# Eight small products moved into the scan's levels, two norms and one product order rearranged, and a small PSUM bank at two bank changes

## The chip, the cores and the metric

The kernel runs on one core of a Trainium2 chip. The metric is device time in microseconds (us) of one execution. Engines are named as in the profile: PE (TensorE, matmuls), PEld (its weight loads), DVE (VectorE), ACT (ScalarE), POOL (GpSimd) and SP (SyncE, whose queue carries most of the DMAs).

## The reference

One layer of a hybrid decoder for 1040 prompt tokens (16 learned meta tokens and 1024 more) and 8 sample tokens, all in float32, with model width 1024:

```
h += 0.5 * SwiGLU_1(rmsnorm(h))            # D_FF = 2816
u  = rmsnorm(h) @ w_in                     # columns shared by two groups of heads
HGRN2, 4 heads, key and value dim 128:
    f = lb + (1-lb) sigmoid(u_f); k = 1 - f; v = u_i; q = silu(u_q)
    S_t = diag(f_t) S_{t-1} + k_t v_t^T;   o_t = S_t^T q_t
    per-head RMSNorm(o) * silu(u_g)
Mamba-2, 8 heads of dim 64, state 128: conv(4) + SiLU, SSD scan, grouped RMSNorm
h += concat(hgrn_out, ssm_out) @ w_out
h += 0.5 * SwiGLU_2(rmsnorm(h))
y  = rmsnorm(h)
```

Outputs are y for prompt and samples and the new states of both groups. Each of the 8 samples has one token and a state of its own, so that its o is one 128x128 by 128x1 product per head.

## The kernel before

Every float32 product is made of three matmuls of split operands: each operand is a high part and a low remainder, and `mm3` issues high by high (L163), high by low (L164) and low by high (L165). PE's order is the order of the program in most of the kernel; in out_proj, and in the last head's norm before it, a scheduler places the instructions of all engines.

PSUM has eight banks. Four are small work banks (`K.psm()`, "mis" in the profile) and four are for accumulation (`K.psum()`, "acc"). In the second half of each FFN (`down`) the accumulation banks are used in twos for six of seven products and, for the last product, one by one, after `K.banks(1)`; the first box of that last product is the place called the bank change.

Both FFNs use a scheme of seven products of blocks in place of eight. `Blocks` makes the operands: `scaled` applies the norm's weight (ACT, L335), `sum_` adds blocks, `cast` makes the high part (ACT, L346), and `low` the remainder (DVE, L352). `w.hi` and `w.lo` (L462, L466), or `w.split` for both, do the same for weights. What is made when, beside which matmul, is written by hand: `before(S, n, ...)` puts calls ahead of step n of the pair of products that is being worked on, and the list which `first2` returns is the order of the seven products. L674, L676, L678, L683, L685 and L689 combine the products' banks.

`hgrn_scan` computes one head. It works through levels m = 1, 2, 4, 8, 16, 32 and 64; at each level there are small matmuls of m or 16 columns (L1758 at levels 32 and 64), then DVE's work for the next level, and then `fill(5)`, which puts five `mm3`, 15 wide matmuls of the next projections, into PE's order. The sample states are loaded and updated in two groups of four (`samples`, at levels 2 and 16). At the head's end PE does 16 output matmuls (L1854, L1856), two for the last 16 tokens (L1860, L1861) and the eight sample products (L1864), which share their bank `po8`. `hgrn_out` then takes the bank's contents as pieces: a square by ACT (L1875), the product with the gate by DVE (L1881), and the norm. For the last head the norm's column sums are matmuls with ones (L1890), taken out of their bank by ACT (L1891), and `rstd_wide` (L194 to L204) makes the root. L1893 applies it.

`out_proj` goes over 8 row tiles and 2 quarters of the tokens for each half of the tokens and each half of the operands: 12 matmuls per tile, a sum on DVE (L1912), and, where `after` is given, a square by ACT (L229) and a sum by POOL (L230) for FFN2's norm. Weights are split by L157 and L158. `Norm.end` (L237 and L173 to L185) finishes the norm of one quarter; `begin_half` (L254 to L256) and `finish` (L259 to L264) do it for two quarters together.

Of the kernel before, what the change touches and what calls it, by code (L numbers as in the profile page):

```python
# [17 lines left out]
P = 128  # L18
# [298 lines left out]
class Blocks:  # L317
# [7 lines left out]
        self.b[p] = self.K.slot("u", self.K.T)  # L325
        return self.b[p]

    def scaled(self, h, wcol, ps):

        for p in ps:  # L330
            k0, n = {1: (0, 0), 7: (0, 1), 2: (4, 0), 3: (4, 1)}[p]
            q = 2 * self.half + n
            t = self.new(p)
            for k in range(4):
                self.K.nc.scalar.activation(t[:, k * self.K.Q : k * self.K.Q + self.K.Q], h[k0 + k][:, q * self.K.Q : q * self.K.Q + self.K.Q], AF.Identity, scale=wcol[:, k0 + k : k0 + k + 1])  # L335

    def sum_(self, p):
# [517 lines left out]
def down(K, S, wdv, hidden, src, h, after):  # L855
# [82 lines left out]
    for a, p in enumerate(DORDER):  # L938
        b = s0 + 24 * a
        if a == 0:  # L940
            at = [b + k for k in (-14, -11, -11, -9, -9, -7)], [b + k for k in (-8, -7, -6, -5, -4, -2)]
        else:
            at = [b - 22 + 3 * m for m in range(6)], [b - 16 + 3 * m for m in range(6)]
        op = hidden.load(S, p, at)
        if a < 6:
            for j in range(KT // 2):
                box = []
                for g in range(3):
                    pieces(p, j, g, b + 6 * j + 2 * g, None)
                    for c in range(2):  # L950

                        def mm(p=p, j=j, g=g, c=c, op=op, box=box):
                            if not box:
                                box.append(K.psum2()[:, :, :K.Q])
                            matmuls(p, j, g, c, op, box[0][:, c])

                        S.add(mm, (lambda p=p, j=j, box=box: post(p, j, slice(0, 2), box[0])) if (g, c) == (2, 1) else None)
        else:
            S.before(b, lambda: K.banks(1))
            then = after(S, h, b - 48 + 24, b + 12, b + 24)  # L960
            for j in range(KT // 2):
                for g in range(3):

                    pieces(p, j, g, b + 3 * j + g, None if j < 2 else "u", (0, 0, 1, 2, 3, 4)[3 * j + g] if j < 2 else 0)
            for c in range(2):
                for j in range(KT // 2):
                    box = []
                    for g in range(3):

                        def mm(p=p, j=j, g=g, c=c, op=op, box=box):  # L970
                            if not box:
                                box.append(K.psum()[:, :K.Q])
                            matmuls(p, j, g, c, op, box[0])

                        S.add(mm, (lambda p=p, j=j, c=c, box=box: post(p, j, slice(c, c + 1), box[0][:, None])) if g == 2 else None)
# [696 lines left out]
def hgrn_scan(K, a, o, hd, u, fill):  # L1672
# [70 lines left out]


    load(0)
    copies, copies8 = [diagonal], [small_diagonal]
    fe = f
    for li, m in enumerate(LEVELS):
        nb = 64 // m
        w = TP if m < 16 else 1024  # L1750
        ps = K.psm()
        qv = qf[:, :1024].rearrange("p (c b s i) -> p c b s i", c=8, s=2, i=m)
        if m >= 32:

            for c in range(8):
                for b in range(nb):
                    r = slice(2 * m * b, 2 * m * b + m)
                    nc.tensor.matmul(ps[r, m * c : m * c + m], kg[:, P * c + 2 * m * b : P * c + 2 * m * b + m], qv[:, c, b, 1], start=True, stop=True)  # L1758
            for b in range(nb):
                r = slice(2 * m * b, 2 * m * b + m)  # L1760
                nc.scalar.copy(pv[r, :, 2 * m * b + m : 2 * m * b + 2 * m], ps[r, : 8 * m].rearrange("p (c i) -> p c i", c=8))
        else:
            nb = 16 // m
            for c in range(8):
                for j in range(4):
                    r = slice(32 * j, 32 * j + 32)
                    nc.tensor.matmul(ps[r, 16 * c : 16 * c + 16], kg[:, P * c + 32 * j : P * c + 32 * j + 32], qv[:, c, nb * j : nb * j + nb, 1], start=True, stop=True)  # L1767

            def copy(m=m, nb=nb, ps=ps):
                pvm = pd.rearrange("p c (b s i) -> p c b s i", s=2, i=m)[:, :, :, 1]  # L1770
                nc.vector.copy_predicated(pvm, K.mask[m].rearrange("p (b i) -> p b i", i=m)[:, None].broadcast_to([P, 8, nb, m]), ps[:, :P].rearrange("p (c b i) -> p c b i", c=8, i=m))
                if m == 16:
                    for r in range(0, P, 32):
                        nc.scalar.copy(pv[r : r + 32, :, r : r + 32], pd[r : r + 32])

            copies.append(copy)
        if li == 0:
            s8 = K.psm()
            nc.tensor.matmul(s8[:16, 64:80], kg[:, 1024:TP], q[:, 1024:TP], start=True, stop=True)
        if m < 16:  # L1780
            q8 = qf[:, 1024:TP].rearrange("p (b s i) -> p b s i", s=2, i=m)
            nc.tensor.matmul(s8[:16, 8 * li : 8 * li + 8], kg[:, 1024:TP], q8[:, :, 1], start=True, stop=True)

            def copy8(li=li, m=m):
                nc.vector.copy_predicated(p8.rearrange("p (b s i) -> p b s i", s=2, i=m)[:, :, 1], K.mask[m][:16, 0:8].rearrange("p (b i) -> p b i", i=m), s8[:16, 8 * li : 8 * li + 8].rearrange("p (b i) -> p b i", i=m))

            copies8.append(copy8)
        n = w // (2 * m)
        fv = fe[:, : w // m].rearrange("p (b s) -> p b s", s=2)
        qw = qf[:, :w].rearrange("p (b s i) -> p b s i", s=2, i=m)  # L1790
        kw = kg[:, :w].rearrange("p (b s i) -> p b s i", s=2, i=m)
        mid = 512 // (2 * m)
        for bs in (slice(0, mid), slice(mid, n)):
            k = bs.stop - bs.start
            nc.vector.tensor_mul(qw[:, bs, 1], qw[:, bs, 1], fv[:, bs, 0:1].broadcast_to([P, k, m]))
            nc.vector.tensor_mul(kw[:, bs, 0], kw[:, bs, 0], fv[:, bs, 1:2].broadcast_to([P, k, m]))
        fn = fp.tile([P, n])
        nc.vector.tensor_mul(fn, fv[:, :, 0], fv[:, :, 1])
        if m == 8:
            f16 = fn  # L1800
        fe = fn
        for copy in copies:
            copy()
        copies = []
        if m == 8:
            for copy in copies8:
                copy()
        if m == 4:
            load(4)
        if m in (2, 16):  # L1810
            samples({2: 0, 16: 4}[m])
        fill(5)
# [47 lines left out]
    nc.tensor.matmul(po8[:, 0:16], vt8, p8, start=True, stop=False)  # L1860
    nc.tensor.matmul(po8[:, 0:16], ss[:, 7], qf[:, 1024:TP], start=False, stop=True)  # L1861

    for b in range(NS):
        nc.tensor.matmul(po8[:, 16 + b : 17 + b], states[b // 4 * 4][:, b % 4], qs[:, b : b + 1], start=True, stop=True)  # L1864
    pieces.append((po8, 1024 - NM, 24))
    return pieces


def hgrn_out(K, hd, pieces, g, tag, fill):
# [12 lines left out]
    if hd < 3:  # L1882
        fill(14)
        next(steps, None)
    else:
        fill(5)
        for ps, c0, w in pieces:
            cs = slice(c0, c0 + w)
            pr = K.psum()
            nc.tensor.matmul(pr[:, :w], K.ones[1], v[:, cs], start=True, stop=True)  # L1890
            an = nc.scalar.activation(v[:, cs], pr[:, :w], AF.Identity, scale=1.0 / P, bias=K.eps)  # L1891
        rstd_wide(K, v, r, an)
# [146 lines left out]
def body(ctx, tc, a, o):  # L2039
# [200 lines left out]
    def keep2(half):  # L2240
        for k in range(KT):
            cs = slice(half * 2 * K.Q, half * 2 * K.Q + 2 * K.Q)
            nc.sync.dma_start(hd2[k][:, cs], h[k][:, cs])

    def after2(k, q):
        nf2.add(k, q)
        if k == KT - 1 and q < 2:
            nf2.end(q)
            if q == 1:
                keep2(0)  # L2250

    out_proj(K, a, h, 1, opb, 0, after2)
    out_proj(K, a, h, 0, opa, 1)
    out_proj(K, a, h, 1, opb, 1, after2)
    ops2 = [Blocks(K, i) for i in range(2)]

    def first2(S, w):
# [29 lines left out]
        e.sum_(5)  # L2287
        e.low(1)
        e.cast(5)
        w.split(2)  # L2290
        e.low(5)
        w.split(6)
        w.split(7)
        w.split(3)
        before(S, 1, (e.scaled, h, wn2, (2,)))
        before(S, 2, (e.scaled, h, wn2, (3,)), (e.cast, 2))
        before(S, 3, (e.sum_, 6), (e.low, 2), (nf2.begin_half, 1))
        before(S, 4, (e.cast, 6), (e.sum_, 7))
        before(S, 5, (e.low, 6), (e.cast, 7))
        before(S, 6, (e.low, 7), (e.sum_, 4), (e.cast, 3))  # L2300
        before(S, 7, (nf2.finish, (1, 1)))
        before(S, 8, (e.low, 3), (e.cast, 4))
        before(S, 9, (w.hi, 4))
        before(S, 10, (e.low, 4), (keep2, 1), (w.lo, 4))
        return 1, 5, 2, 6, 7, 3, 4

    def after3(S, h, e3, e0, e1):
        nf = []
# [55 lines left out]
```

## Time and profile before

| | us |
|---|---|
| median of 3 runs | 1956.12 |
| lowest and highest | 1952.58, 1958.87 |
| profiled execution | 1959.24 |
| its span | 1957.5 |

The profile is of one execution; times in it count from the span's start. PE is the busiest engine by far. In the lists, `x` gives the number of instruction records (a float32 matmul on 32-bit operands may leave two), and the clock is what was granted to TensorE, as a share of full speed. FFN1 lies up to about 690 us, the four heads' scans lie between 930 and 1170 us, out_proj from 1174 to 1276 us, and FFN2 follows.

### The profile page before, as it was taken

To read this page: it belongs to the slowest core of one execution; us is meant where nothing else is said; L and a number is where in the kernel's file an instruction comes from. 1 tells how busy PE (TensorE), PEld (TensorE's weight loads), DVE (VectorE), ACT (ScalarE), POOL (GpSimd) and SP (SyncE) were. 2 spreads that over 40 slices of the span, in tenths; PEclk is the share of its full clock that TensorE was granted. 3 is DMA by queue.
4 is the path that set the end of the run, shared out by engine and by line. 5 is a ranking of instruction groups with operands and counts; after the bars stand their busy time and mean duration, and the time that the engine had idled before them with its cause. 6 is when DMAs were issued, how large, how long until landed. Compare 5 with 4: busy or idle time off the path is not lost.

```text
span 1957.5 us, 41043 instructions
## 1 busy us (share of the span) xinstructions
PE 1917.1 (98%) x16569; PEld 1883.5 (96%) x16569; DVE 1532.7 (78%) x2783; ACT 850.3 (43%) x1632; POOL 91.5 (5%) x155
## 2 busy tenths in 40 slices
PE   7999999999999999999999999999999999999997
PEld 6999999999999999999999999999999999999997
DVE  7788888888788867576765657888888888878965
ACT  7533233333533644466644535742332323354353
POOL 4000000000000410000000001200000000000000
PEclk9999999999999999999999999999999999999999
DMA  7223333335977551221641454224332333587862
GB/s 222 77 88 109 93 99 105 100 97 161 283 234 251 158 159 51 66 87 44 177 122 52 124 172 135 77 82 120 92 109 87 103 104 104 161 245 233 271 194 77
DMA packets 324646, 260.59 MB, mean 133 GB/s; under 512 B 17824, under 2 KB 299680, under 8 KB 324448
## 3 DMA queue, kind: packets, MB, share of 16 engines
q1 hardware_dynamic: 324216, 257.92, 43.5%
q8 instruction: 131, 2.15, 0.5%
q14 instruction: 59, 0.48, 0.1%
q0 software_dynamic: 224, 0.04, 0.0%
q10 hardware_dynamic: 16, 0.00, 0.0%
HBM read 192.90 MB, written 65.07 MB: 132 GB/s over the span
## 4 chain that ended last, share of the span: by engine, by line
PE 86%; DVE 7%; DMA 2%; ACT 2%; issue 1%; SPq 0%; POOL 0%; DVEq 0%; ACTq 0%; POOLq 0%
PE acc L163 26%; PE acc L165 25%; PE acc L164 25%; PE mis L163 1%; PE mis L165 1%; PE mis L164 1%; DVE u L352 1%; DVE ws L466 1%; DMA s<-in_x_prompt_dram 1%; DMA r<-in_w_ffn_up_dram 1%; DVE r L458 1%; PE mis L1767 1%; DMA s<-cumd 1%; PE mis L1835 0%; DVE t L669 0%
## 5 line engine op out<-in xcount | busy, mean ns | idle before, releaser
L163 PE MATMUL acc<-u,ws 128*128 128x258 f32 (+3 forms) x4248 | 1243.1, 293 | 7.5 <-DVE t L683 2.5
L164 PE MATMUL acc<-u,ws 128*128 128x258 f32 (+3 forms) x4248 | 1233.2, 290 | 4.4 <-DVE u L352 4.0
L165 PE MATMUL acc<-u,ws 128*128 128x258 f32 (+3 forms) x4248 | 1232.6, 290 | 3.3 <-DVE ws L466 3.3
L163 PEld LDWEIGHTS acc<-u,ws 128*128 128x128 f32 x4248 | 805.1, 190 | 12.9 <-issue 3.6
L164 PEld LDWEIGHTS acc<-u,ws 128*128 128x128 f32 x4248 | 807.5, 190 | 6.9 <-DVE u L352 5.0
L165 PEld LDWEIGHTS acc<-u,ws 128*128 128x128 f32 x4248 | 804.9, 189 | 4.7 <-DVE ws L466 4.6
L466 DVE TENSOR_TENSOR ws<-r,ws 128x512 fp32r<-128x512 f32 x276 | 190.9, 693 | 75.0 <-ACT ws L462 74.9
L462 ACT CAST ws<-r 128x512 fp32r<-128x512 f32 x276 | 160.1, 615 | 12.9 <-ACT ws L462 7.7
L458 DVE TENSOR_TENSOR r<-r,r 128x512 f32<-128x512 f32 x176 | 120.9, 689 | 4.8 <-DMA r<-in_w_ffn_up_dram 3.3
L681 ACT ACTIVATE t<-t 128x516 f32<-128x516 f32 (+1 forms) x41 | 26.2, 639 | 213.3 <-DVE t L669 213.3
L712 ACT ACTIVATE t<-t 128x524 f32<-128x524 f32 (+1 forms) x47 | 29.9, 639 | 196.3 <-DVE t L669 196.3
L846 DVE TENSOR_TENSOR u<-u,u 128x1048 fp32r<-128x1048 f32 (+3 forms) x84 | 97.0, 1157 | 5.5 <-ACT u L842 5.5
L669 DVE TENSOR_TENSOR t<-t,u 128x524 f32<-128x524 f32 (+1 forms) x135 | 92.9, 697 | 2.9
L158 DVE TENSOR_TENSOR ws<-r,ws 128x512 fp32r<-128x512 f32 x88 | 60.6, 699 | 42.2 <-ACT ws L157 41.9
L230 POOL TENSOR_TENSOR t<-t,t 128x262 f32<-128x262 f32 (+1 forms) x56 | 54.4, 982 | 812.5 <-ACT t L229 708.5
L903 ACT CAST ws<-u 128x512 fp32r<-128x512 f32 (+1 forms) x72 | 42.2, 586 | 102.2 <-DVE u L898 92.1
L842 ACT CAST u<-u 128x1048 fp32r<-128x1048 f32 (+3 forms) x84 | 82.9, 989 | 0.0
L932 DVE SCALAR_TENSOR_TENSOR s<-acc,s 128x524 f32<-128x524 f32 (+3 forms) x88 | 54.6, 643 | 31.7 <-PE acc L165 31.4
L903 ACT CAST ws<-r 128x512 fp32r<-128x512 f32 (+1 forms) x84 | 47.9, 582 | 70.8 <-DVE r L898 29.5
L908 DVE TENSOR_TENSOR ws<-r,ws 128x512 fp32r<-128x512 f32 (+1 forms) x84 | 57.4, 693 | 23.2 <-ACT ws L903 23.1
L157 ACT CAST ws<-r 128x512 fp32r<-128x512 f32 x88 | 53.9, 617 | 36.5 <-PE acc L165 30.6
L908 DVE TENSOR_TENSOR ws<-u,ws 128x512 fp32r<-128x512 f32 (+1 forms) x72 | 47.4, 658 | 26.5 <-ACT ws L903 26.5
(435 smaller groups left out, 2290.7 us busy)
## 6 DMA issues: line engine op xcount, KB each, us to landing
r<-in_w_ffn_down_dram SPq DMA_DIRECT2D x128, 256.0 KB
hd<-s SPq DMA_DIRECT2D x93, 258.0 KB
r<-in_w_ffn_gate_dram SPq DMA_DIRECT2D x88, 256.0 KB
r<-in_w_ffn_up_dram SPq DMA_DIRECT2D x88, 256.0 KB
hd<-s SPq DMA_DIRECT2D x77, 262.0 KB
u<-hd SPq DMA_DIRECT2D x36, 516.0 KB
u<-hd SPq DMA_DIRECT2D x28, 524.0 KB
r<-in_w_in_dram SPq DMA_DIRECT2D x56, 256.0 KB
```

What stands on the lines that cost most here:

```text
L158: self.nc.vector.tensor_sub(lo, src, hi.bitcast(F32))
L163: mm(ps, whi, xhi, start=first, stop=False, skip_group_check=more)
L164: mm(ps, whi, xlo, start=False, stop=False, skip_group_check=more)
L165: mm(ps, wlo, xhi, start=False, stop=last, skip_group_check=more)
L458: self.K.nc.vector.tensor_tensor(self.raw[p], self.raw[x], self.raw[y], op)
L462: self.K.nc.scalar.copy(self.w[p][:, : self.n * P], self.raw[p])
L466: self.K.nc.vector.tensor_sub(t[:, 512 : 512 + w], self.raw[p], t[:, :w].bitcast(F32))
L669: nc.vector.tensor_mul(t, t if src is None else src, spread.lanes(i, cs))
L842: K.nc.scalar.copy(hi, lo.bitcast(F32))
L846: K.nc.vector.tensor_sub(lo, lo.bitcast(F32), hi.bitcast(F32))
L903: nc.scalar.copy(w[p, j, g][:, : n * P], src)
L908: nc.vector.tensor_sub(t[:, 512 : 512 + n * P], box[0], t[:, : n * P].bitcast(F32))
```

## The change

There are five parts. The eight sample products are done by a new function `outputs(b0)` in two groups of four, behind the matmuls of level 32 and of level 64, each group in a small bank of its own, and ACT copies them to a tile `os8` in SBUF; `hgrn_out` then has four pieces in place of three. In the last head's norm the ones-matmuls write to small banks. FFN2's norm for the first half of the tokens is begun and finished for both quarters together, inside the next call of out_proj. FFN2's first pair has another product order, its scalings can be made in parts (`ks`), and some splits stand at other steps. The first box of the last product in `down` uses a small bank.

```diff
-    def scaled(self, h, wcol, ps):
+    def scaled(self, h, wcol, ps, ks=range(4)):
...
-            t = self.new(p)
-            for k in range(4):
+            t = self.new(p) if 0 in ks else self.b[p]
+            for k in ks:
...
-                                box.append(K.psum()[:, :K.Q])
+                                box.append((K.psum() if c or j else K.psm())[:, :K.Q])
...
     load(0)
+    os8 = small("os8", P, NS)
+
+    def outputs(b0):
+        ps = K.psm()
+        for i in range(4):
+            nc.tensor.matmul(ps[:, i : i + 1], states[b0][:, i], qs[:, b0 + i : b0 + i + 1], start=True, stop=True)
+        nc.scalar.copy(os8[:, b0 : b0 + 4], ps[:, 0:4])
+
...
+        if m >= 32:
+            outputs({32: 0, 64: 4}[m])
         n = w // (2 * m)
...
-    for b in range(NS):
-        nc.tensor.matmul(po8[:, 16 + b : 17 + b], states[b // 4 * 4][:, b % 4], qs[:, b : b + 1], start=True, stop=True)
-    pieces.append((po8, 1024 - NM, 24))
+    pieces.append((po8, 1024 - NM, 16))
+    pieces.append((os8, TP - NM, NS))
...
-            pr = K.psum()
+            pr = K.psm()
             nc.tensor.matmul(pr[:, :w], K.ones[1], v[:, cs], start=True, stop=True)
...
     def after2(k, q):
         nf2.add(k, q)
-        if k == KT - 1 and q < 2:
-            nf2.end(q)
-            if q == 1:
-                keep2(0)
+        if (k, q) == (KT - 1, 1):
+            keep2(0)
+
+    def norm2(k, q):
+        if (k, q) == (0, 3):
+            nf2.begin_half(0)
+        elif (k, q) == (1, 2):
+            nf2.finish((0, 0))
 
     out_proj(K, a, h, 1, opb, 0, after2)
-    out_proj(K, a, h, 0, opa, 1)
+    out_proj(K, a, h, 0, opa, 1, norm2)
     out_proj(K, a, h, 1, opb, 1, after2)
...
+        w.split(6)
+        e.low(5)
+        e.scaled(h, wn2, (2,), (0, 1))
         w.split(2)
-        e.low(5)
-        w.split(6)
-        w.split(7)
-        w.split(3)
-        before(S, 1, (e.scaled, h, wn2, (2,)))
-        before(S, 2, (e.scaled, h, wn2, (3,)), (e.cast, 2))
-        before(S, 3, (e.sum_, 6), (e.low, 2), (nf2.begin_half, 1))
+        e.scaled(h, wn2, (2,), (2,))
+        before(S, 1, (e.scaled, h, wn2, (2,), (3,)), (w.hi, 7), (e.scaled, h, wn2, (3,), (0, 1)), (w.lo, 7))
+        before(S, 2, (w.hi, 3), (e.scaled, h, wn2, (3,), (2, 3)), (e.cast, 2))
+        before(S, 3, (w.lo, 3), (e.sum_, 6), (e.low, 2), (nf2.begin_half, 1))
...
-        before(S, 6, (e.low, 7), (e.sum_, 4), (e.cast, 3))
-        before(S, 7, (nf2.finish, (1, 1)))
+        before(S, 6, (e.low, 7), (e.sum_, 4))
+        before(S, 7, (e.cast, 3), (nf2.finish, (1, 1)))
...
-        return 1, 5, 2, 6, 7, 3, 4
+        return 1, 5, 6, 2, 7, 3, 4
```

How the instructions stand now is shown at three places, in each engine's own order; line numbers of the changed kernel are some 8 to 13 higher in these functions (L1864, L1866, L1870 and L1871 are the old L1854, L1856, L1860 and L1861).

PE at the end of a head (the third), before: the output matmuls in bank 13391, then those of `po8` (13400), `qs` being the samples' q and `r` their states.

```order
L1854 MATMUL mis_13391<-s_12838,s_12796 128x128
L1856 MATMUL mis_13391<-s_12794,s_13315 128x128
L1860 MATMUL mis_13400<-p_1606_12840,vt_1598_12797 128x16
L1861 MATMUL mis_13400<-s_12794,s_13315 128x16
L1864 MATMUL mis_13400<-qs_12818,r_12877 128x1 x4
L1864 MATMUL mis_13400<-qs_12818,r_13047 128x1 x4
L163 MATMUL acc_13367<-u_8461,ws_13124 128x350
```

PE at level 64 of the same head in the changed kernel: L1766 is the level's own matmul, L1751 the sample product.

```order
L165 MATMUL acc_13223<-u_8461,ws_12795 128x350
L1766 MATMUL mis_13272<-s_12808,u_12042 64x64 x8
L1751 MATMUL mis_13282<-qs_12832,r_13062 128x1 x4
L163 MATMUL acc_13223<-u_8462,ws_12795 128x350
L164 MATMUL acc_13223<-u_8470,ws_12795 128x350
```

The four products of the second group have moved from the end of the head to a place between the level's matmuls and the wide ones of the filling; the first group stands in the same way at level 32.

PE at the last head's norm, before: L163 to L165 into bank 14165 are the last projection, those into bank 14268 the first tile of out_proj.

```order
L165 MATMUL acc_14165<-u_8463,ws_13508 128x344
L1890 MATMUL acc_14224<-u_14216,ones_83 128x496
L1890 MATMUL acc_14227<-u_14216,ones_83 128x512
L1890 MATMUL acc_14230<-u_14216,ones_83 128x24
L163 MATMUL acc_14268<-u_13567,ws_14260 128x258
```

The same norm in the changed kernel (L1899); bank 14327 is out_proj's third tile.

```order
L165 MATMUL acc_14327<-u_13588,ws_14291 128x258
L1899 MATMUL mis_14252<-u_14242,ones_83 128x496
L163 MATMUL acc_14327<-u_13830,ws_14291 128x258
L164 MATMUL acc_14327<-u_13831,ws_14291 128x258
L165 MATMUL acc_14327<-u_13830,ws_14291 128x258
L163 MATMUL acc_14327<-u_14018,ws_14296 128x258
L1899 MATMUL mis_14255<-u_14242,ones_83 128x512
L1899 MATMUL mis_14258<-u_14242,ones_83 128x16
L164 MATMUL acc_14327<-u_14019,ws_14296 128x258
```

The ones-matmuls, which stood ahead of all of out_proj, now come after its first 27 matmuls and between later ones.

ACT at FFN2's first pair, before: L674 and L678 copy banks that PE has filled, L335 scales a block of 258 tokens, and L346 casts.

```order
L674 COPY t_15589<-acc_15576 128x258
L335 ACTIVATE u_15591<-s_14250,col 128x258
L335 ACTIVATE u_15591<-s_14252,col 128x258
L335 ACTIVATE u_15591<-s_14254,col 128x258
L335 ACTIVATE u_15591<-s_14256,col 128x258
L335 ACTIVATE u_15609<-s_14250,col 128x258
L335 ACTIVATE u_15609<-s_14252,col 128x258
L335 ACTIVATE u_15609<-s_14254,col 128x258
L335 ACTIVATE u_15609<-s_14256,col 128x258
L346 CAST u_15614<-u_15591 128x1032
L678 COPY t_15628<-acc_15576 128x258
```

ACT there in the changed kernel; L462 casts weights, and 15591 and 15616 are the blocks that were 15591 and 15609.

```order
L335 ACTIVATE u_15591<-s_14285,col 128x258
L674 COPY t_15611<-acc_15598 128x258
L335 ACTIVATE u_15591<-s_14287,col 128x258
L462 CAST ws_15614<-r_15494 128x512
L335 ACTIVATE u_15616<-s_14281,col 128x258
L335 ACTIVATE u_15616<-s_14283,col 128x258
L462 CAST ws_15633<-r_15560 128x512
L335 ACTIVATE u_15616<-s_14285,col 128x258
L335 ACTIVATE u_15616<-s_14287,col 128x258
L346 CAST u_15637<-u_15591 128x1032
```

Three of the eight scalings now stand ahead of the first copy L674, and the casts of two weights between the others.

## The prediction, made before the changed kernel ran

> **What bounds the kernel now.** I read the page first. The profiled execution took 1959.24 us, and its span is 1957.5 us, so 1.7 us lie outside the span; the median of the three timed runs, 1956.12 us, lies 3.1 us below this execution.
>
> ```profile
> span 1957.5 us, 41043 instructions
> PE 1917.1 (98%) x16569; PEld 1883.5 (96%) x16569; DVE 1532.7 (78%) x2783; ACT 850.3 (43%) x1632; POOL 91.5 (5%) x155
> ```
>
> TensorE (PE) is busy in 1917.1 of 1957.5 us, so all that can be had without dropping matmuls is the 40.4 us in which it stands still, and whatever makes the matmuls themselves slow. A change that leaves the products as they are, as this one does, can act on nothing else. For the second kind I cut the ends of the four HGRN2 heads into windows and read the granted clock. Columns: window, length, PE busy (records), clock as a share of full speed, DMA share, GB/s.
>
> ```profile
> 964.45:967.86 3.41, 3.41 (x14) 0.50 1.02 272
> 1056.60:1060.01 3.41, 3.41 (x24) 1.00 0.02 5
> 1107.81:1111.22 3.41, 3.41 (x14) 0.50 0.12 47
> 1159.00:1162.42 3.42, 3.42 (x31) 1.00 0.77 233
> 1162.42:1165.83 3.41, 3.41 (x14) 0.50 1.02 401
> 1165.83:1169.24 3.41, 3.41 (x23) 1.00 1.01 396
> ```
>
> Three of the four heads are followed by one window of 3.41 us at half clock. The starts stand on one grid: 1107.81 - 964.45 is 42.0 windows and 1162.42 - 1107.81 is 16.0. The timeline of PE around the same four ends (start, duration, operation) shows what precedes them.
>
> ```profile
> 961.99 0.39 PE L1860 MATMUL mis<-p,vt 16*128 16x16 f32 x2
> 964.34 0.54 PE L163 MATMUL acc<-u,ws 128*128 128x344 f32 x1
> ...
> 1054.54 0.39 PE L1860 MATMUL mis<-p,vt 16*128 16x16 f32 x2
> 1056.89 0.40 PE L163 MATMUL acc<-u,ws 128*128 128x344 f32 x1
> ...
> 1104.99 0.39 PE L1860 MATMUL mis<-p,vt 16*128 16x16 f32 x2
> 1107.35 0.40 PE L163 MATMUL acc<-u,ws 128*128 128x350 f32 x1
> ...
> 1160.18 0.39 PE L1860 MATMUL mis<-p,vt 16*128 16x16 f32 x2
> 1160.75 2.03 PE L1864 MATMUL mis<-qs,r 128*128 128x1 f32 x16
> 1162.64 0.63 PE L163 MATMUL acc<-u,ws 128*128 128x344 f32 x1
> ...
> 1163.65 0.49 PE L163 MATMUL acc<-u,ws 128*128 128x344 f32 x1
> 1164.51 0.49 PE L163 MATMUL acc<-u,ws 128*128 128x344 f32 x1
> ...
> 1166.06 0.32 PE L163 MATMUL acc<-u,ws 128*128 128x344 f32 x1
> 1166.53 0.32 PE L163 MATMUL acc<-u,ws 128*128 128x344 f32 x1
> ```
>
> From L1860 to the next wide matmul PE does only products 1 or 16 columns wide, for 2.35 us (961.99 to 964.34; 2.35, 2.36 and 2.46 in the others). The wide matmuls left in the window ahead of the half-clock one fill 3.41 less the narrow stretch inside it: 961.04 to 961.99 and 964.34 to 964.45 make 1.06 us in head 0; 1.05 in head 2; 1159.00 to 1160.18 make 1.18 in head 3. In head 1 the grid cuts the stretch at 1056.60: the window from 1053.19 has 1.35 us of wide matmuls, and no half clock follows. So in these four a window with up to 1.18 us of wide work cost the clock, and one with 1.35 did not. The price: three matmuls take 0.86 us at half clock (1163.65 to 1164.51) and 0.47 at full (1166.06 to 1166.53), so a window of 3.41 us does the work of 1.86 and costs 1.55 us.
>
> **The change, part by part.**
>
> *Sample products at two levels.* The eight products (16 records of L1864, some 1.8 us of PE) leave the head's end; four go behind level 32's matmuls and four behind level 64's. PE's work is the same. What stands there now, in head 3:
>
> ```profile
> 1141.89 0.70 PE L1758 MATMUL mis<-s,u 128*32 128x32 f32 x32
> 1142.52 0.43 PE L163 MATMUL acc<-u,ws 128*128 128x344 f32 x1
> ...
> 1145.09 1.15 PE L1758 MATMUL mis<-s,u 128*64 128x64 f32 x16
> 1146.16 0.42 PE L163 MATMUL acc<-u,ws 128*128 128x344 f32 x1
> ```
>
> The narrow stretches become 0.63 + 0.9 = 1.5 us at level 32 and 1.07 + 0.9 = 2.0 us at level 64, with 2.57 us of wide matmuls between them (1142.52 to 1145.09). A window that holds all of the longer stretch still has 3.41 - 2.0 = 1.4 us of wide work, just above the 1.35 that kept the clock. At the head's end only L1860 and L1861, 0.6 us, are left. So I expect no half-clock window at these places: 3 x 1.55 = 4.7 us off this execution. What it adds is per head two ACT copies of 128x4, one more ACT square and one more DVE product 8 columns wide; each stands right behind work of the same level and hides beside the wide matmuls, and its price without that cover is some 0.3 us a head. Bounds: -4.7 us, or 0 where the half clock only moves.
>
> *Last head's norm in small banks.* This and the next part are in the waits of PE between 1160 and 1260 us (what waits, for what: sum, times, longest):
>
> ```profile
> PE acc L1890 <- ACT u L1875: 2.9, 1, 2.9
> PE mis L237 <- POOL t L230: 0.8, 2, 0.6
> ```
>
> The ones-matmuls L1890 sit ahead of out_proj in PE's order and wait 2.9 us for a square. With small banks the first of them comes after 27 matmuls of out_proj, so this wait goes. What is late next is DVE, in the windows view (PE, PEld, DVE, ACT, POOL busy, then clock) and in the rows at the start of its chain:
>
> ```profile
> 1175.50:1190.50 15.00, 12.68 (x100) 12.21 (x101) 14.46 (x20) 10.91 (x19) 0.00 (x0) 1.00 0.24 72
> ...
> 1170.77 0.60 ACT L1875 ACTIVATE u<-mis 128x496 f32<-128x496 f32 x1
> ...
> 1175.54 1.23 DVE L202 TENSOR_TENSOR s<-s,s 128x1032 f32<-128x1032 f32 x1 [3.40 <-ACT s L201]
> ```
>
> DVE is busy 14.46 of 15.00 us here, and at the end of that stretch stands the split of out_proj's third pair of weights (L158), for which PE will now wait, having run ahead. It comes earlier only by what the chain in front of L202 loses, one square of 0.60 us that now stands behind the table load, so I take -0.6 us; the ends are 0 and the whole -2.9.
>
> *FFN2's first norm in one step.* Each L237 waits for the last POOL sum of its quarter; for the first quarter the chain is:
>
> ```profile
> 1223.88 0.42 DVE L1912 TENSOR_TENSOR s<-s,acc 128x258 f32<-128x258 f32 x1 [1.02 <-PE acc L165]
> ...
> 1224.40 0.42 ACT L229 ACTIVATE t<-s 128x258 f32<-128x258 f32 x1 [1.02 <-DVE s L1912]
> 1224.83 1.28 ACT L173 ACT_TABLE_LOAD   x1
> ...
> 1224.96 0.73 POOL L230 TENSOR_TENSOR t<-t,t 128x258 f32<-128x258 f32 x1 [0.70 <-ACT t L229]
> ...
> 1225.74 0.70 PE L237 MATMUL mis<-t,ones 128*128 128x258 f32 x2 [0.58 <-POOL t L230]
> ```
>
> From the end of PE's tile (1223.84) to L237 that is 1.9 us. After the change both ones-matmuls stand 24 matmuls, or 2.9 us at 0.12 each, behind the second quarter's last tile, so both sums are in time, and without a table load between them: -0.8 us. Were the POOL sum 1.0 us later, 0.2 of it would come back; bounds -0.8 and +0.5.
>
> *FFN2's first pair.* Waits of PE from 1270 to 1300 us, the load of the engines, and the ACT row that causes most of it:
>
> ```profile
> PE acc L163 <- ACT t L674: 1.4, 2, 0.9
> PE acc L163 <- DVE t L683: 1.0, 1, 1.0
> ...
> 1273.00:1300.00 27.00, 24.22 (x190) 23.08 (x189) 24.45 (x37) 14.97 (x30) 3.38 (x4) 1.00 0.29 100
> ...
> 1276.79 3.32 ACT L335 ACTIVATE u<-s,col 128x258 f32<-128x258 f32 x8
> ```
>
> Eight scalings stand in one block of 3.32 us behind the first L674 copy, and the cast and the copy L678 that PE waits for stand behind that block. The change puts three of the eight ahead of the pair's first step and the others in ones and twos between the weights' casts, lets product 6 take the place of 2, and spreads the splits of weights 7 and 3 over the first steps. PE stands still for 27.00 - 24.22 = 2.8 us here. DVE's 24.45 us of work stays, so the stretch cannot lose more than 27.00 - 24.45 = 2.55 us. Following the new order through with these durations, the three waits go and one of about 0.9 comes back in the second half, at L683 behind the norm's finish on DVE: -1.8 us, ends -0.5 and -2.5.
>
> *Small bank at both bank changes.* From the waits of the whole run:
>
> ```profile
> PE acc L163 <- DVE s L932: 1.8, 2, 0.9
> ```
>
> At each change to single banks the first box waits 0.9 us until DVE has emptied a double bank. A small bank is free at that point, and the second box comes 12 matmuls later, which is longer than the wait: -1.8 us, at worst -1.0.
>
> **Sum.** -4.7 - 0.6 - 0.8 - 1.8 - 1.8 = -9.7: 1959.24 becomes 1949.5. The median needs another route, as the grid falls anew in each execution: a narrow stretch of 2.4 us leaves at most 1.25 us of wide work (between 1.18 and 1.35) in some 40% of its positions, or 1.6 of the four heads on average. That is 2.5 us, and 1956.12 - 2.5 - 5.0 is 1948.6. I take **1949.0 us**.
>
> **Rivals.**
>
> *The clock gains nothing.* The row of 1159.00 shows PE busy 3.42 of 3.42 us, and the next window at half clock, so it is not standing still that costs the clock here. If the half-clock windows have another cause than these products, or follow them to level 64, only the other four parts count: 1956.1 - 5.0 = 1951.1, up to 1954.2 against this execution. For it: 1.4 against 1.35 us is a thin margin. Against it: the three out of four, and the grid. The Trainium skill (TensorE: Matmul & The Clock Gate, Part 1) says that the clock falls after at least one idle window of about 3.4 us, and that the window runs free; the free grid agrees with this trace, but by the idle rule there would have been no half clock here at all, and the three windows at 0.50 behind a busy PE speak against it. By that rule the first part is worth nothing.
>
> *DVE takes the waits over.* With 14.46 of 15.00 and 24.45 of 27.00 us busy it may give the second and fourth part nearly nothing (-0.3 together). Then 1959.24 - 4.7 - 0.3 - 0.8 - 1.8 = 1951.6, or 1950.7 by the median's route. For it speaks that both orders were worked through by hand with old durations.
>
> *Half clock at both levels, in every head.* Were the limit not 1.35 but some 2 us of wide work, as the four ends alone cannot exclude for stretches of 32- and 64-column matmuls, levels 32 and 64 would each cost a window in each head: 8 x 1.55 = 12.4 us. That turns the gain into a loss as soon as four windows come (4 x 1.55 = 6.2 against 2.5 + 5.0 = 7.5, five at the latest); with eight the time is 1956.1 - 7.5 + 12.4 = 1961.0. Against it: level 64's 1.07 us stand there today, and no half clock follows at 1146.
>
> *The change does not do what it says.* If the two waits at the bank changes and those of L237 stayed (-2.6 less), the time would be 1951.6.
>
> **Chances.** The forecast as worked out has 0.57, the clock without gain 0.17, DVE taking over 0.15, half clock at the levels 0.05, the undone change 0.03, anything else 0.03. 0.3%, or 5.9 us, is about what a measurement of this kernel can tell from no change: faster means below 1950.2, slower above 1962.0. The forecast lies below that line in some 85 of 100 cases and the next two in 35, which gives 0.60; slower is a part of the last cases only, 0.05; the same has 0.35. The range runs from all gains at their best (1949.0 less 2.3 for the second, 0.7 for the fourth part and 1.5 for one half-clock window elsewhere: 1944.5) to the rivals without gain plus one such window more (1956.0).
>
> **What would show it.** Right: clock 1.00 in all windows behind the heads' ends; no wait of PE at the last head's ones-matmuls and at the bank changes; none for POOL at L254's matmuls; a new wait of 1.5 to 2.5 us for L158 and for DVE's sums in the first third of out_proj; one of about 0.9 us for L683 in FFN2's first pair. Wrong: windows at 0.50 behind levels 32 or 64, a longer wait for DVE behind L1902's chain, or a time above 1956.

## The result, and the profile after

The changed kernel takes 1950.62 us (median of 10 runs, 1947.13 to 1953.68); the kernel before, run beside it, 1956.31 (10 runs, 1952.15 to 1960.04). The ratio is 0.9969, with a 95% interval from 0.9957 to 0.9980: 3.9 to 8.4 us less. The profiled execution took 1951.22 us.

The top of the page of the changed kernel:

```profile
span 1949.5 us, 41056 instructions
PE 1913.9 (98%) x16571; PEld 1881.7 (97%) x16571; DVE 1533.0 (79%) x2785; ACT 850.4 (44%) x1642; POOL 90.8 (5%) x155
```

Of the 8.0 us between the two spans PE's busy time gives 3.2 and its standing still the rest (40.4 us before, 35.6 now). Not all of it is the change's: the first sum of FFN1's second half on DVE (L932) already comes 3.2 us earlier (at 526.3 against 529.5 us), after a stretch that both programs have alike; 1.5 us of that are two waits of PE for DVE between 60 and 480 us that the execution of before shows and that of the changed kernel does not.

The ends of the four heads in the changed kernel (window, length, PE busy, clock, DMA share, GB/s), where three of four windows had been at half clock:

```profile
955.00:975.00 20.00, 20.00 (x137) 1.00 0.62 175
1044.00:1064.00 20.00, 20.00 (x263) 1.00 0.01 4
1097.00:1117.00 20.00, 20.00 (x138) 1.00 0.26 86
1151.00:1171.00 20.00, 19.93 (x131) 1.00 0.48 171
```

All are at full clock, as forecast. Inside a head the changed kernel still has one half-clock window, from 1015.35 us, behind a stretch of 16-column matmuls (L1775) in which PE stands still for 1.8 us; the kernel before has such a window in the same stretch, from 1022.47 us (L1767), and the change does not touch it. The waits of PE from out_proj's start to the end of FFN2's first pair, where before it waited 2.9 us at L1890, 0.8 at L237 and 2.4 in the pair:

```profile
PE acc L163 <- DVE t L683: 2.2, 1, 2.2
PE acc L165 <- DVE ws L158: 1.2, 1, 1.2
PE acc L163 <- DVE s L1921: 0.9, 1, 0.9
```

The waits at the ones-matmuls, for POOL, and at the two bank changes (1.8 us) are gone. In their place stand 1.2 + 0.9 = 2.1 us in out_proj and one wait of 2.2 us in the pair. In this profile both new ones also cost clock; the windows on the grid around them:

```profile
1179.19:1182.60 3.41, 1.56 (x11) 1.00 0.00 0
1182.60:1186.01 3.41, 3.16 (x14) 0.50 0.53 159
1281.59:1285.00 3.41, 1.20 (x10) 1.00 0.00 0
1285.00:1288.41 3.41, 3.41 (x18) 0.50 0.26 77
```

PE worked 1.56 and 1.20 us of the first and third window, and each is followed by one at half clock. Whether that happens depends on how the grid cuts the wait: the kernel without the sample products (below) has the wait at L683 too, 2.3 us long, and keeps the clock there. What PE waits for in the pair is seen in DVE's rows:

```profile
1279.78 0.68 DVE L259 SCALAR_TENSOR_TENSOR t<-t 128x516 f32<-128x516 f32 x1
1280.50 0.76 DVE L262 SCALAR_TENSOR_TENSOR t<-mis,t 128x258 f32<-128x258 f32 x2
1281.29 0.70 DVE L264 SCALAR_TENSOR_TENSOR u<-t,t 128x516 f32<-128x516 f32 x1
1281.90 1.23 DVE L352 TENSOR_TENSOR u<-u,u 128x1032 fp32r<-128x1032 f32 x1
1283.05 0.42 DVE L676 TENSOR_TENSOR t<-acc,t 128x258 f32<-128x258 f32 x1
1283.50 0.42 DVE L683 TENSOR_TENSOR t<-acc,t 128x258 f32<-128x258 f32 x1
```

The norm's finish (L259 to L264) and the remainder of product 3's operand (L352) stand on DVE ahead of L676 and L683, which empty the bank that PE needs. In out_proj it is the same with the last head's norm:

```profile
1180.97 1.22 DVE L1902 TENSOR_TENSOR u<-u,u 128x1032 f32<-128x1032 f32 x1
1182.12 2.49 DVE L158 TENSOR_TENSOR ws<-r,ws 128x512 fp32r<-128x512 f32 x4
```

The split of the third pair of weights (L158) comes behind the gate's product (L1902), the last of that chain.

### The profile page after: what moved, and what is told of

Read it like the earlier page. It is cut to its first block, busy times and chain, and to the rows that moved or that the text cites. A ratio compares the mean times of both kernels' runs of the same rounds, so it can differ in the third digit from the quotient of the medians.

```text
span 1949.5 us, 41056 instructions
## 1 busy us (share of the span) xinstructions
PE 1913.9 (98%) x16571; PEld 1881.7 (97%) x16571; DVE 1533.0 (79%) x2785; ACT 850.4 (44%) x1642; POOL 90.8 (5%) x155
## 4 chain that ended last, share of the span: by engine, by line
PE 89%; DVE 6%; ACT 1%; issue 1%; DMA 1%; SPq 0%; DVEq 0%; POOL 0%; ACTq 0%; POOLq 0%
PE acc L163 26%; PE acc L165 26%; PE acc L164 26%; PE mis L163 2%; PE mis L165 2%; PE mis L164 1%; DVE u L352 1%; DVE u L341 1%; DVE ws L466 1%; PE mis L1452 0%; PE mis L1775 0%; PE mis L1845 0%; PE mis L1448 0%; DMA s<-in_x_prompt_dram 0%; PE mis L1751 0%
## 5 line engine op out<-in xcount | busy, mean ns | idle before, releaser
L163 PE MATMUL acc<-u,ws 128*128 128x258 f32 (+4 forms) x4226 | 1235.7, 293 | 5.6 <-DVE t L683 2.2
L165 PE MATMUL acc<-u,ws 128*128 128x258 f32 (+4 forms) x4226 | 1226.3, 290 | 4.7 <-DVE ws L466 3.4
L164 PE MATMUL acc<-u,ws 128*128 128x258 f32 (+4 forms) x4226 | 1225.3, 290 | 2.9 <-DVE u L352 2.5
L163 PEld LDWEIGHTS acc<-u,ws 128*128 128x128 f32 x4226 | 800.3, 189 | 9.8 <-issue 4.3
L165 PEld LDWEIGHTS acc<-u,ws 128*128 128x128 f32 x4226 | 799.3, 189 | 6.2 <-DVE ws L466 4.7
L466 DVE TENSOR_TENSOR ws<-r,ws 128x512 fp32r<-128x512 f32 x276 | 190.2, 690 | 75.7 <-ACT ws L462 75.6
L462 ACT CAST ws<-r 128x512 fp32r<-128x512 f32 x276 | 160.1, 614 | 14.4 <-ACT ws L462 7.8
L158 DVE TENSOR_TENSOR ws<-r,ws 128x512 fp32r<-128x512 f32 x88 | 60.8, 700 | 44.8 <-ACT ws L157 44.7
L932 DVE SCALAR_TENSOR_TENSOR s<-acc,s 128x524 f32<-128x524 f32 (+3 forms) x86 | 53.8, 648 | 30.3 <-PE acc L165 30.0
```

What stands on the lines that cost most here:

```text
L158: self.nc.vector.tensor_sub(lo, src, hi.bitcast(F32))
L163: mm(ps, whi, xhi, start=first, stop=False, skip_group_check=more)
L164: mm(ps, whi, xlo, start=False, stop=False, skip_group_check=more)
L165: mm(ps, wlo, xhi, start=False, stop=last, skip_group_check=more)
L462: self.K.nc.scalar.copy(self.w[p][:, : self.n * P], self.raw[p])
L466: self.K.nc.vector.tensor_sub(t[:, 512 : 512 + w], self.raw[p], t[:, :w].bitcast(F32))
```

## The experiments

Each kernel was timed beside the kernel before; ratios are to it. Theory A: the clock halves behind a window of 3.41 us in which PE streams too few columns (streaming a column means passing it through the array; a matmul of one column takes PE's time, 0.11 us per record, but streams almost nothing). Its rival B: only a window of standing still does that. Theory C: the order on DVE makes the two new waits. Its rival D: DVE is the bound of these stretches whatever the order.

### The sample products alone

```diff
 (the kernel before, and of the change only:)
+        if m >= 32:
+            outputs({32: 0, 64: 4}[m])
```

> The kernel before with the first part of the change alone: the eight sample products behind levels 32 and 64. Theory A (a window of 3.41 us with too little wide work costs the clock in the next): no window at 0.50 behind the four heads' ends; 1.6 such windows fewer on average, 1956.3 - 2.5 = 1953.8 us. Theory B (only a window in which PE stands idle costs the clock): nothing changes, 1956.3 us. Both: the waits of PE elsewhere as before (2.9 us at L1890, 0.8 at L237, 1.8 at the bank changes).

Measured: 1954.99 us (12 runs), 0.9990 [0.9979, 1.0002]. The windows at the four heads' ends are at 1.00, as A says; 1.8 us is less than A's 2.5, and the interval, -4.1 to +0.4 us, holds both A and no change. The time alone does not decide here. One thing went against the expectation that the other waits stay as they were: the wait at the last head's ones-matmuls (L1890, here L1899) grew from 2.9 to 3.3 us,

```profile
PE acc L1899 <- ACT u L1884: 3.3, 1, 3.3
```

and in this profile a half-clock window follows it, from 1170.98 us, where the trace of before had none.

### All of the change but the sample products

```diff
-        if m >= 32:
-            outputs({32: 0, 64: 4}[m])
...
+    for b in range(NS):
+        nc.tensor.matmul(po8[:, 16 + b : 17 + b], states[b // 4 * 4][:, b % 4], qs[:, b : b + 1], start=True, stop=True)
```

> The changed kernel without its first part: the sample products stand at the heads' ends again, the other four parts are kept. Theory A: windows at 0.50 behind the sample products in one to three of the four heads, 1950.6 + 2.5 = 1953.1 us. Theory B: as the changed kernel, 1950.6 us.

Measured: 1950.55 us (12 runs), 0.9969 [0.9954, 0.9984], the same as the changed kernel. The windows at the heads' ends:

```profile
955.00:975.00 20.00, 20.00 (x131) 0.91 0.73 206
1045.00:1065.00 20.00, 20.00 (x143) 1.00 0.01 4
1097.00:1117.00 20.00, 20.00 (x141) 1.00 0.24 84
1151.00:1171.00 20.00, 20.00 (x136) 1.00 0.64 226
```

One head has its half-clock window again, so B's mechanism does not hold even here: PE is busy 20.00 of 20.00 us. But the loss in time that A expected is not there, and by the time alone the first part brings nothing in the changed kernel. The waits from 1160 to 1260 us of this kernel give a part of the reason:

```profile
PE acc L163 <- DVE s L1912: 1.0, 1, 1.0
```

They are 1.0 us where the changed kernel has 2.1. With the sample products at the last head's end PE begins out_proj 4.2 us later than in the changed kernel (first L163 at 1169.61 against 1165.40 us), but the last step of DVE's chain there, the gate's product, ends only 2.3 us later (1184.38 against 1182.12 us). The products thus stand where PE would otherwise wait for DVE; moved ahead, they make this wait longer, and in the profile of the changed kernel it is long enough to bring the clock down. So part of the first part's gain is given back in out_proj. How much of it, the times do not tell: the two intervals are some 5 us wide.

### All eight products behind level 64

```diff
-        if m >= 32:
-            outputs({32: 0, 64: 4}[m])
+        if m == 64:
+            outputs(0)
+            outputs(4)
```

> The changed kernel with all eight sample products behind level 64 and none behind level 32: the same work, but a narrow stretch of 1.07 + 1.8 = 2.9 us in place of 2.0. Theory A: a window at 0.50 behind level 64 in two or three of the four heads, 1950.6 + 2.5 x 1.55 = 1954.5 us. Theory B: no window at 0.50 there, 1950.6 us.

Measured: 1949.73 us (6 runs), 0.9958 [0.9943, 0.9974]; theory A as stated there fails. The level's own matmuls and the eight products, in the third head, and the clock of 20 us around them:

```profile
1081.21 1.15 PE L1766 MATMUL mis<-s,u 128*64 128x64 f32 x16
1082.28 1.95 PE L1751 MATMUL mis<-qs,r 128*128 128x1 f32 x16
...
1078.00:1098.00 20.00, 20.00 (x182) 1.00 0.24 65
```

The other three heads are at 1.00 too. The stretch is 2.9 us long, longer than those at the heads' ends before, and the clock stays. What was wrong is the count of level 64's matmuls as narrow: 16 records in 1.07 us are 0.067 us each for 64 columns of float32. At the pace of L1854 and L1856 (0.11 us per record of 128 columns) 64 columns need 0.055 us, some 0.83 of that. They stream most of the time; only single columns don't.

With that the windows of the profiles fall in order. I counted each matmul with the time that its columns need: the Trainium skill (TensorE: Matmul & The Clock Gate, Part 1) gives N / 2.4 GHz for N columns and a fixed 2.5 ns, which I left out. The trace nearly agrees: 350 columns come every 0.16 us, where this gives 0.15. For float32 I took twice N / 2.4 GHz for each of the two records (0.107 us for 128 columns, where L1854 and L1856 take 0.11), and where records overlap I counted the time once. By this estimate the windows ahead of a half clock at the heads' ends hold 0.91 to 1.18 us of streaming (six windows: three of before, one of the kernel just above and two of the last kernel below), those of the two new waits 1.01 and 0.85; the window ahead of head 1's boundary of before, which kept the clock, holds 1.25. I did the same for every window of the grid between 60 and 1930 us in all twelve profiles. Outside the Mamba-2 part, every window with 1.24 us or less is followed by half clock, none with 1.30 or more is, and between 1.25 and 1.29 both occur. So the limit is near 1.3 of 3.41 us by this count. The places behind levels 32 and 64 in the changed kernel leave 2.0 us, wherever the grid falls.

The row of eight products behind level 64 is not shown to be safe. Slid over the trace of this kernel, a window holds as little as 1.18 us there, and less than 1.3 in 0.19 of the positions; four heads without a half clock, as here, would then come in some 0.4 of the executions.

### The products doubled, at the ends and at the levels

```diff
 (at the ends, on the kernel without the first part:)
-    for b in range(NS):
+    for b in [*range(NS), *range(NS)]:
 (at the levels, on the changed kernel:)
-        for i in range(4):
+        for i in [*range(4), *range(4)]:
```

At the ends:

> The changed kernel with its sample products at the heads' ends again, and each of them done twice into the same place: 4 x 1.79 = 7.2 us more work for PE, and a narrow stretch of 2.35 + 1.79 = 4.1 us. Theory A, with the limit now read from six traces (the clock halves behind a window of 3.41 us in which columns stream for less than 1.3 us; 32 and 64 columns of float32 count as work, single columns do not): one window at 0.50 behind each of the four heads, 6.2 us more than the kernel with doubled products at the levels. Theory B (only an idle window costs the clock): the same time as that kernel, 1957.8 us.

At the levels:

> The changed kernel with each sample product done twice where it stands, behind levels 32 and 64: the same 7.2 us more work for PE, in eight stretches of 1.8 us. Both theories: 1950.6 + 7.2 = 1957.8 us, and no window at 0.50 behind the levels, since 3.41 - 1.8 = 1.6 us are left for wide work.

Measured: 1968.02 us (7 runs), 1.0057 [1.0036, 1.0077], at the ends; 1964.12 us (12 runs), 1.0032 [1.0017, 1.0046], at the levels. At the ends all four heads have a half-clock window, two of them two in a row (window, length, PE busy, clock, DMA share, GB/s):

```profile
950.00:970.00 20.00, 20.00 (x125) 0.83 0.63 178
1046.00:1066.00 20.00, 20.00 (x125) 0.83 0.01 4
1104.00:1124.00 20.00, 20.00 (x135) 0.91 0.25 84
1165.00:1185.00 20.00, 20.00 (x132) 0.91 0.60 214
```

At the levels I expected no such window and 7.2 us; it cost 12.3 us by the ratios (13.5 by the medians). The third head there, the products and the grid's windows:

```profile
1087.72 0.70 PE L1766 MATMUL mis<-s,u 128*32 128x32 f32 x32
1088.34 1.95 PE L1751 MATMUL mis<-qs,r 128*128 128x1 f32 x16
...
1087.37:1090.78 3.41, 3.41 (x55) 1.00 0.69 184
1090.78:1094.20 3.42, 3.42 (x13) 0.50 0.17 51
```

PE is busy for the whole window and the next is at half clock; five of the eight levels in this profile have one. 1.8 us of single columns and 0.63 us of level 32 leave 1.0 us for wide work, which I had left out of the count: by the same estimate these five windows hold 1.12 to 1.27 us, and the three at the levels that kept the clock 1.28, 1.45 and 1.62. The changed kernel has the same instructions there but for the doubled products, and no half clock behind any of its eight levels. This is what shows that the products cause it, wherever they stand, and that B is wrong: standing still plays no part in these windows. Between the two kernels A expected 6.2 us and 3.9 were measured; the intervals overlap a little. The second one has such windows too: in the profiled executions 5 at the levels, against 6 at the ends.

### FFN2's first pair in its old order

```diff
-        return 1, 5, 6, 2, 7, 3, 4
+        return 1, 5, 2, 6, 7, 3, 4
 (and the steps of the pair as before)
```

> The changed kernel with FFN2's first pair in its old order (1, 5, 2, 6, 7, 3, 4, scalings in one block). Theory C (the new order moved three waits of 2.4 us together into one of 2.2 us, behind which the clock often halves): no slower than the changed kernel, 1950 to 1951 us, with the three waits of 0.5, 1.0 and 0.9 us back. The prediction's own step (a gain of 1.8 us): 1952.4 us.

Measured: 1949.92 us (8 runs), 0.9959 [0.9944, 0.9975]: not slower than the changed kernel (0.9969), and the intervals overlap. The waits in this stretch are back as they were:

```profile
PE acc L163 <- ACT t L674: 1.7, 2, 0.9
PE acc L163 <- DVE t L683: 1.0, 1, 1.0
```

2.7 us in three places do not cost more than 2.2 in one place, which can bring the clock down. The new order by itself brought nothing that can be measured.

### The two waits attacked

In the first kernel the finish of FFN2's second norm goes from step 7 to step 11, and the last head's root and gate product are written behind the tenth of out_proj's tiles (row tile 4, second quarter):

```diff
-        before(S, 7, (e.cast, 3), (nf2.finish, (1, 1)))
+        before(S, 7, (e.cast, 3))
...
+        before(S, 11, (nf2.finish, (1, 1)))
...
-        rstd_wide(K, v, r, an)
+        def tail():
+            rstd_wide(K, v, r, an)
+            nc.vector.tensor_mul(g, g, r)
+
+        return tail
...
-    out_proj(K, a, h, 0, opa, 0)
+    out_proj(K, a, h, 0, opa, 0, lambda k, q: tail() if (k, q) == (4, 1) else None)
```

> The changed kernel with its two new waits attacked: the finish of FFN2's second norm (four DVE instructions, 2.1 us) is put ahead of step 11 in place of step 7, and the last head's root and gate product are written behind out_proj's first nine tiles. Theory C (the order on DVE made the waits of 2.2 us at L683 and of 0.9 and 1.2 us in out_proj, and each pulled a half-clock window behind it): both waits go but for some 0.4 us, and the half-clock windows at 1182 and 1285 with them; 1950.6 - 3.9 - (1 to 2) x 1.4 gives 1944 to 1946 us. Theory D (DVE is the bound of both stretches, the order only says where PE waits): the waits turn up a few us later in the same sum, 1950 to 1951 us.

Measured: 1949.28 us (6 runs), 0.9953 [0.9937, 0.9969]. This misses C's 1944 to 1946. The waits in out_proj are gone, so C holds there. In the pair D looked right: the waits turned up later, 2.5 us in all, the largest of them

```profile
PE acc L163 <- DVE t L689: 1.4, 1, 1.4
```

behind the finish at its new place, and with a half-clock window from 1286.01 us. In the second kernel the finish goes to step 13, behind the last sum that PE waits for (L689), and all else stays as in the first:

> The changed kernel with the last head's root and gate product written behind out_proj's first nine tiles, and the finish of FFN2's second norm at step 13 of 14. Theory C: no wait in out_proj's first third, and in the pair only 0.3 to 1.0 us in place of 2.2, without a half-clock window behind; 1950.6 - 2.1 - 1.5 - (1 to 2) x 1.2 gives 1945 to 1946 us. Theory D (DVE bounds the pair): some 2.5 us of waits remain in the pair in other places; 1948 to 1949 us.

Measured: 1945.99 us (6 runs), 0.9942 [0.9921, 0.9963]. Waits of PE from 1160 to 1295 us:

```profile
PE acc L165 <- DVE ws L466: 1.1, 2, 0.9
PE acc L163 <- DVE t L683: 0.3, 1, 0.3
PE mis L163 <- DVE t L685: 0.2, 1, 0.2
```

That is 1.6 us in all where the changed kernel has 4.3, and no half-clock window from the first head up to the kernel's last 6 us. In out_proj nothing is left to wait for: DVE had room there, and its order had been at fault. All of the 1.6 us are in the pair. That is more than C's 0.3 to 1.0 and less than D's 2.5: at L683 2.2 us became 0.3, but PE now waits 0.9 us for a split of weights (L466) some steps later. In the pair the order decides where PE waits and in how many pieces, and the clock with it; that DVE's amount of work does not bound this stretch is not shown.

### The repaired kernel with and without the sample products

> The repaired kernel once more, beside its twin without the first part: 1946 to 1947 us, no wait of PE in out_proj's first third, under 1 us in the pair, and no half-clock window between the first head and the end.

> The repaired kernel without the first part of the change: the sample products at the heads' ends, and behind them nothing that waits for DVE. Theory A: a window at 0.50 behind each head's end in 53 of 100 executions (from the share of positions of the grid that leave less than 1.3 us of streaming in a window), so 2.1 windows x 1.5 = 3.2 us slower than the repaired kernel, 1949 to 1950 us. Theory B (only an idle window costs the clock): the same time as the repaired kernel.

Measured: 1946.28 us (5 runs), 0.9954 [0.9940, 0.9968], with the products at the levels; 1947.84 us (10 runs), 0.9960 [0.9944, 0.9975], with them at the ends. The waits of PE in the first are those of the run before, 1.6 us in the pair, where under 1 us was expected. The difference of 1.6 us has the forecast sign and half its size, and the intervals overlap, so the times do not settle what the first part is worth. The windows show that the half clock is there: two of the four heads of the second kernel are followed by it, none of the first.

Over all the profiles: with the eight products at the heads' ends, once each, 6 of 12 ends are followed by a half-clock window (3 in the kernel before, 1 and 2 in the two kernels without the first part); with the products at the levels, none of 28 ends in seven kernels. Sliding a window over every position around a head's end that stays at full clock (head 1 of before, heads 1 and 2 of the two others), with 1.3 us as the limit, gives 0.53 per head, 2.1 windows per execution; at 1.55 us each the first part would be worth 3.2 us by this estimate. No pair of runs has shown as much: 1.8 us alone, nothing in the change as made, 1.6 in the repaired kernel, each within its noise.

## Why the prediction was right, and which terms were off

The time, 1950.62 us against 1949.0 forecast, lies in the range, and the change is faster. By its steps:

- **Sample products.** The mechanism stands: no half-clock window follows a head's end, and the doubled products show the cause. The reason given for the margin was wrong: 32- and 64-column matmuls were counted with the single columns, "1.4 against 1.35 us", where it is 2.0 against 1.3. The rival that put half clock at both levels in every head is answered by the trace: none of the eight levels has one. The average of 1.6 windows was low; the estimate is now 2.1. The 2.5 us taken for them in the time are not shown: without this part the changed kernel takes the same time. That part of the gain in the last head goes back to a wait for DVE was not seen.
- **Last head's norm.** -0.6 us was forecast; 2.9 us of waiting became 2.1, or -0.8, with the waits for DVE's sums and for L158 that were named. Not in the sum: whether the clock halves behind such a wait. In the trace of before the 2.9 us happened to be cut by the grid and cost no clock (with the first part alone the same wait did); in the trace after, the 2.1 us cost a window.
- **First norm in one step.** -0.8 us forecast, and no wait for POOL is left there.
- **First pair.** This term failed. "The three waits go and one of about 0.9 comes back" should have read 2.2: L352 for product 3 stands on DVE behind the four instructions of the finish, and both are ahead of L676 and L683. 2.8 us of waits became 2.2, with a half-clock window behind them in the profiled execution, where -1.8 us had been forecast; the kernel with the old order is no slower. The rival that DVE takes the waits over describes this stretch. Moving the four instructions took the wait at L683 down to 0.3 us, but 1.6 us stayed in the pair, so how much of it is DVE's order and how much its amount of work is open.
- **Bank changes.** -1.8 us forecast; both waits are gone.

The sum was 1.6 us too good, and that it came so near is in part luck. Of the 7.5 us on the median's route the sample products (2.5) and the pair (1.8) brought nothing that the runs can see in the changed kernel. The waits that did go (0.8, 0.8 and 1.8) make 3.4 of the 5.7 us measured; what the other 2.3 us are, about half the width of the interval, is not shown. The range had to hold the half-clock windows that come and go with the grid, and it did.

## What to carry to other kernels

Add up the work of a wait's window as well as the wait: several short waits can be cheaper than one that leaves little streaming in 3.41 us, because the next window then runs at half clock (here some 1.5 us more). Rows of single-column products should be kept short and set among wide matmuls, so that no window is left with less than some 1.3 us of streaming; here 2.35 us of products of 1 and 16 columns were enough to cost the clock at half of the heads' ends. Where PE waits for DVE, look first at what stands ahead of that instruction in DVE's order and has no reader yet: here moving two such pieces brought the kernel to 1946 us against 1950.6, 3 to 5 us more by the ratios of two measurements, though the intervals still overlap.

## What the hardware showed that was not expected

A PE that is busy for all of a window can lose half its clock: the window at 1087.37 in the kernel with the doubled products is busy 3.41 of 3.41 us. By the estimate above the limit is at 1.25 to 1.3 us of streaming in 3.41, and matmuls of one column, at 0.11 us each, add next to nothing. The Trainium skill (TensorE: Matmul & The Clock Gate, Part 1) names an idle window as the condition; these profiles do not agree with that. Three windows outside the heads, in the Mamba-2 part of the kernel, lost the clock at 1.4 us (half clock from 759.35 us in the changed kernel) and 1.8 us (half clock from about 905 us in the two kernels with the products at the ends, once each) by the same count; how their matmuls should be counted is left open.
